# Attention scores issued two steps ahead, with another order and another pace of the projection products between them

## The chip, the cores and the metric

The kernel runs on one core of a Trainium2 chip. The time is the device time of one execution in microseconds (us); of several runs the median counts. The engines are named as in the profile: PE (TensorE matmuls), PEld (its weight loads), DVE (VectorE), ACT (ScalarE), POOL (GpSimd), SP (SyncE, which here only issues DMAs). Each engine works through its own instructions in the order in which they stand.

## The reference, cut to what matters

One attention layer and then one convolution layer over 1024 latent tokens with 1024 channels, plus 256 context tokens. The attention layer, which the change is in, has 16 query heads in 4 groups; the 4 heads of a group share one key and one value head of width 128:

```python
proj = h_lat @ w_in                                   # q | k | v | z
q = apply_rope(split_heads(proj[..., :q_end], 16), cos, sin)
k = apply_rope(split_heads(proj[..., q_end:k_end], 4), cos, sin)
# block of 128 queries: keys of the blocks before, at and after it (|i-j| <= 128), all 256 context keys, a sink
p_ctx, p_win = sink_softmax(sink_l, s_ctx, s_win)
o = p_ctx @ vc + p_win @ vw
y = (o * jax.nn.silu(z)) @ w_out
```

Everything is f32. The kernel splits each f32 operand into a high and a low part and makes each product of three matmuls (high with high, high with low, low with high).

## The kernel before, in words

**Stages.** The kernel first normalises and modulates the tokens and projects head 0 (to about 110 us of the profile), then runs the attention loop (to about 890 us), then the output projection, the convolution layer and the final norm. PE's order is the order of the code, instruction by instruction. The order on DVE, ACT, POOL and SP is set by a scheduler when the kernel is built, which also picks which of two PSUM buffers a `pss` tile gets.

**A step.** The loop walks over 128 steps (h, b): head h of 16, query block b of 8. Three pieces of PE work belong to a step, and I write them S, T and pv:

- S(h, b), `scores`: six matmuls `pss<-kh/kl/kvc,qh/ql` that need the rotated queries `qh`, `ql` of head h. Behind them come DVE (the masked maximum, `CUSTOM_DVE ... p_page<-pss`), ACT (`exp`), DVE (reciprocal) and POOL (the scaling), which leave the probabilities in a page `p`.
- T(h, b), `transposes`: up to five transposes `pss<-ident,p_page`, which ACT and DVE copy out as `pthi` and `ptlo`.
- pv(h, half), `pv`: 21 matmuls `pso<-pthi/ptlo,...` after every fourth block. DVE multiplies the result by the gate `zs` of that half.

Before, step (h, b) issues S of the next step, then 12 filler products, then pv if one is due, then T(h, b). So a score is issued one step ahead of its transposes.

**Filler products.** A filler product is one 128x512 matmul `psg<-hh/hl,whi/wlo` of the projection of a later head. A "chunk" is 128 columns of `w_in`, two halves of 512 tokens, 24 products each. Chunk z(h) makes the gate of head h, chunk q(h) its queries. A half of q is not ready when its products are: `rope` copies it out on ACT, two DMAs on ACT's queue swap its halves, POOL and DVE multiply and add, ACT writes `qh`, POOL writes `ql`. Each chunk's weights come by one 512 KB DMA into a page `wraw` and are split by ACT (`whi`) and POOL (`wlo`) while the chunk before them is at work.

At the first block of a head the loop enqueues the chunks that the next head needs, and `fill(n)` takes n products from the queue. The first head of a group must take z(h), q(h+1) and also z(h+1), q(h+2); the last enqueues nothing. `fill(1000, ("q", h + 1))` empties the queue up to the next head's queries before that head's first score. At the end of a group ("regroup") the chunks k and v of the next group run in one piece, then S of the new group's first step.

**Other work in the loop.** `low_parts` (`lows`), from head 1 on, loads 512 KB of an output weight per item into a page `low`, has ACT and POOL take its low part (`lhi`, `low_page<-low_page,lhi_half`) and writes it back by DMA. `ada_rest` adds up the modulation vectors of the next layer on DVE (`mask_page`). All pages (`p`, `q`, `z`, weights, `low`) come from one pool of 45, first in, first out; a page handed out again waits for its last reader.

Of the kernel before, what the change touches and what calls it, by code (L numbers as in the profile page):

```python
# [14 lines left out]
P = 128  # L15
# [4 lines left out]
NH = 16  # L20
NG = 4
HD = 128
AW = NH * HD
KW = NG * HD
# [6 lines left out]
TB = T // P  # L31

ADA_FP = ((0, 0),)
FILL = 12
DEFER = 6
EARLY = 2
FIRST = 5
# [57 lines left out]
def backbone_kernel(  # L95
# [154 lines left out]
    def wcol(c0):  # L250
        return W[:, c0:c0 + P]
# [7 lines left out]
    def add_chunk(key, src):  # L259
        cidx[key] = len(chunks)  # L260
        chunks.append(src)
# [1 line left out]
    for key, src in (("k", 0), wk[0]), (("q", 0), wcol(0)), (("v", 0), wv[0]):  # L263
        add_chunk(key, src)
    for h in range(NH):
        add_chunk(("z", h), wcol(AW + 2 * KW + h * P))
        if h + 1 < NH:
            add_chunk(("q", h + 1), wcol((h + 1) * P))
        if h % 4 == 3 and h + 1 < NH:
            add_chunk(("k", h // 4 + 1), wk[h // 4 + 1])  # L270
            add_chunk(("v", h // 4 + 1), wv[h // 4 + 1])
# [526 lines left out]
    def finish(kind, n, half, o, d):  # L798

        sl = slice(half * 512, half * 512 + 512)  # L800
        if kind in "kv" and half == 2:
            c = kvt[n][2]
            if kind == "k":
                act(c[:, 0], o[:, 0:CT], AF.Copy)
                split_lo(V, c[:, 1], o[:, 0:CT], c[:, 0])
                return None
        if kind in "qk":
            return rope(o, sl, d[0][:, sl], d[1][:, sl], G if kind == "q" and n else V)
        if kind == "z":
            act(d[:, sl], o, AF.Tanh, scale=0.5)  # L810
            stt(d[:, sl], d[:, sl], 1.0, o, ALU.add, ALU.mult)
            return None
        w = CT if half == 2 else 512
        f = hp.alloc(F32, None, "vf")
        act(f[:, 0:w], o[:, 0:w], AF.Copy)

        def tail():
            if half == 2:
                vt_split(f, CT, *(c[:, i].rearrange("p (a b) -> p a b", b=P) for i in (2, 3)))
            else:  # L820
                vt_split(f, 512, *(t[:, half * 4:half * 4 + 4] for t in d))
            hp.free(f)

        return tail
# [24 lines left out]
    def job(key):  # L849
        kind, n = key  # L850
        i = cidx[key]
        wc = wsA.need(i)
        d = target(kind, n)
        wsA.load()
        late = None
        for half in PARTS[kind]:
            o = ps_g()
            gh = gemm_ctx(wc, o) if half == 2 else gemm_half(wc, half, o)
            for m, _ in enumerate(gh):
                yield  # L860
                if m == DEFER - 1 and late:
                    late()
            if half == PARTS[kind][0] and wsA.ns <= i + 1:
                wsA.split()
                wsA.load()
            late = finish(kind, n, half, o, d)
        if late:
            vlate[n] = late
        wsA.done(i)
        if key == ("v", NG - 1):  # L870
            for t in Hc:
                pg.free(*t)
# [8 lines left out]
    def fill(n, until=None):  # L881
        while n > 0 and fillq and until not in finished:
            try:
                next(fillq[0][1])
                n -= 1
            except StopIteration:
                finished.add(fillq.popleft()[0])

    def enqueue(key):
        fillq.append((key, job(key)))  # L890
# [56 lines left out]

    def pv(h, half):
        g = h // 4
        c, vh, vl = kvt[g][2:5]  # L950
        o = ps_o()
        q0 = half * 4
        work = [(*(c[:, n, i * P:i * P + P] for n in (2, 3)), slice(13 + 4 * i, 17 + 4 * i), slice(0, 512)) for i in range(2)]
        for kb in range(max(q0 - 1, 0), min(q0 + 4, TB - 1) + 1):
            qa, qz = max(kb - 1, q0), min(kb + 1, q0 + 3)
            b0 = 1 + 4 * (1 - (kb - qa)) + (qa - q0)
            n = qz - qa + 1
            if n == 1 and kb > qa:
                work.append((vh[:, kb], vl[:, kb], slice(0, 5, 4), slice(256, 512)))
            elif n == 1:  # L960
                work.append((vh[:, kb], vl[:, kb], slice(9, 22, 12), slice(0, 256)))
            else:
                work.append((vh[:, kb], vl[:, kb], slice(b0, b0 + 5 * (n - 1) + 1, 5),
                             slice((qa - q0) * P, (qz - q0 + 1) * P)))
        for n, (a, b, ps_, os_) in enumerate(work):
            last = n == len(work) - 1
            PE.matmul(o[:, os_], a, pthi[:, ps_], start=n == 0, stop=False)
            PE.matmul(o[:, os_], a, ptlo[:, ps_], start=False, stop=False)
            PE.matmul(o[:, os_], b, pthi[:, ps_], start=False, stop=last)
        sl = slice(half * 512, half * 512 + 512)  # L970
        oz = hp.alloc(F32, None, "oz")
        stt(oz[:, 0:512], o, 0.5, zt[h][:, sl], ALU.mult, ALU.mult)
        SY.dma_start(out=ozd[h, :, sl], in_=oz[:, 0:512])
        hp.free(oz)
        if half:
            pg.free(zt.pop(h))
            pg.free(*qt.pop(h))
# [45 lines left out]
    steps = [(h, qb) for h in range(NH) for qb in range(TB)]  # L1023
# [6 lines left out]
    tails.pop()()  # L1030
    for _ in range(2):
        next(adag)
    for i, (h, qb) in enumerate(steps):
        if qb == 0:
            for n in (() if h % 4 == 3 else (h + 1,) if h % 4 or not h else (h, h + 1)):
                enqueue(("z", n))
                if n + 1 < NH:
                    enqueue(("q", n + 1))
        if (h, qb) == (NH - 1, EARLY_FROM):
            run(lows)  # L1040
            for _ in range(EA + 1):
                next(projA)
            fillq.append((("wo", 0), early_proj()))
        if lstate[0] == "open" or h and (h % 4 < 3 or qb < LOWS):
            lstate[0] = next(lows, "shut")
        nxt = steps[i + 1] if i + 1 < len(steps) else None
        regroup = nxt and nxt[1] == 0 and nxt[0] % 4 == 0
        if nxt and nxt[1] == 0:
            fill(1000, ("q", h + 1))
        if nxt and not regroup:  # L1050
            scores(*nxt)
        if not regroup:
            fill(FILL)
        if pvq:
            pv(*pvq.popleft())
        if regroup:
            g = nxt[0] // 4
            old = kvt[g - 1]
            run(job(("k", g)))
            transposes(h, qb)  # L1060
            run(job(("v", g)))
            pv(h, 1)
            pg.free(*old)
            scores(*nxt)
            vlate.pop(g)()
            continue
        transposes(h, qb)
        if qb % 4 == 3:
            pvq.append((h, qb // 4))
        for _ in range(2 if qb == 1 or qb == 6 and h % 2 else 1):  # L1070
            next(adag, None)
# [577 lines left out]
```

## Time and profile before

| | us |
|---|---|
| median of 3 runs | 1788.18 |
| lowest and highest run | 1786.36, 1790.24 |
| the profiled execution | 1789.18 |
| its span, first to last instruction | 1787.4 |
| PE busy in the span | 1731.3 |

The profiled execution takes 1.8 us beyond its span, and lies 1.0 us over the median. A row of the timeline has start, duration, engine, line, operation, output `<-` inputs, and in brackets the idle time before it with what ended it. All instructions have line L89, a helper, so the names of the tiles tell the work apart. A matmul's duration overlaps the next one's; the distance between two starts is what a product costs. In a row of windows stand PE busy, PEld, DVE, ACT, POOL, the granted share of the TensorE clock (PEclk), the DMA engines' busy share and GB/s.

### The profile page before, as it was taken

What the parts mean: (1) busy time and instruction counts of PE and PEld (TensorE: products, weight loads), DVE (VectorE), ACT (ScalarE), POOL (GpSimd) and SP (SyncE); (2) the same over time, 40 slices, a digit from 0 to 9 for tenths busy, and PEclk for the clock granted to TensorE, in tenths of its full rate; (3) what the DMA queues carried; (4) which work ended last, traced back from release to release, by engine and by line L of the source; (5) the groups of instructions that cost most, each with busy time, mean ns of one, the idle gap of its engine ahead of it and who ended that gap; (6) DMA issues with size and microseconds to landing.
All of it is one profiled execution on the core that took longest, in us unless ns stands there. A gap on an engine that the chain in (4) does not pass through costs nothing.

```text
span 1787.4 us, 23804 instructions
## 1 busy us (share of the span) xinstructions
PE 1731.3 (97%) x8383; PEld 1428.6 (80%) x8383; DVE 1147.8 (64%) x2078; ACT 866.8 (48%) x1406; POOL 940.5 (53%) x844
## 2 busy tenths in 40 slices
PE   5899999999999999899999999999999999999997
PEld 3578888788887888788888888888888888788886
DVE  5755564556544654455514349999999999867823
ACT  5344443445444544444533435655656565466731
POOL 2345665566644665654200147998988889121300
PEclk8899999999999999899999999999999999999999
DMA  9324443345334443334787723111121212376971
GB/s 302 106 54 124 147 134 89 112 139 162 104 93 140 142 139 101 109 109 145 286 279 248 256 86 112 42 46 37 36 80 39 71 48 70 107 252 231 328 272 47
DMA packets 195324, 242.45 MB, mean 136 GB/s; under 512 B 11798, under 2 KB 126790, under 8 KB 195204
## 3 DMA queue, kind: packets, MB, share of 16 engines
q1 hardware_dynamic: 188516, 230.10, 39.4%
q10 hardware_dynamic: 6688, 10.83, 2.5%
q8 instruction: 66, 1.08, 0.2%
q14 instruction: 54, 0.44, 0.1%
HBM read 188.70 MB, written 41.69 MB: 129 GB/s over the span
## 4 chain that ended last, share of the span: by engine, by line
PE 91%; DMA 3%; DVE 2%; issue 1%; ACT 1%; POOL 1%; SPq 0%; ACTq 0%; POOLq 0%; DVEq 0%
PE psg L89 46%; PE pss L89 23%; PE pso L89 21%; DMA rope_half<-rope_half 1%; DMA low_page<-in_conv_w_out_dram 1%; DVE alo_page L89 1%; SPq L89 0%; DMA araw_page<-in_ada_w_dram 0%; DMA ozd<-oz_half 0%; DVE ptlo L89 0%; DMA ozf_page<-ozd 0%; DMA x_page<-in_x_dram 0%; POOL ql_page L89 0%; DMA low_page<-in_attn_w_out_dram 0%; DVE hf_page L89 0%
## 5 line engine op out<-in xcount | busy, mean ns | idle before, releaser
L89 POOL TENSOR_TENSOR odd_half<-odd_half,prod_half 128x513 f32<-128x513 f32 (+2 forms) x252 | 313.4, 1252 | 24.1 <-ACT prod_half L89 10.9
L89 PE MATMUL psg<-hh_page,whi_page 128*128 128x512 f32 x600 | 240.9, 402 | 0.3 <-DVE kvc_page L89 0.3
L89 PE MATMUL psg<-hh_page,wlo_page 128*128 128x512 f32 x600 | 239.6, 399 | 0.0
L89 PE MATMUL psg<-hl_page,whi_page 128*128 128x512 f32 x600 | 239.4, 399 | 0.0
L89 POOL TENSOR_TENSOR wlo_page<-wraw_page,whi_page 128x1024 fp32r<-128x1024 f32 x72 | 179.6, 2496 | 98.8 <-ACT whi_page L89 74.3
L89 ACT ACTIVATE prod_half<-ubuf,dww 128x513 f32<-128x513 f32 (+2 forms) x252 | 165.1, 675 | 110.6 <-POOL odd_half L89 107.9
L89 PE MATMUL psg<-h2h_page,whi_page 128*128 128x512 f32 x464 | 184.1, 397 | 0.0
L89 PE MATMUL psg<-h2l_page,whi_page 128*128 128x512 f32 x464 | 182.7, 394 | 0.0
L89 PE MATMUL psg<-h2h_page,wlo_page 128*128 128x512 f32 x464 | 182.6, 393 | 0.0
L89 POOL TENSOR_SCALAR p_page<-p_page,sc 128x640 f32<-128x640 f32 (+1 forms) x128 | 101.1, 790 | 149.2 <-DVE sc L89 148.2
L89 DVE SCALAR_TENSOR_TENSOR pss<-ubuf,dww,pss 128x512 f32<-128x512 f32 (+3 forms) x270 | 172.5, 671 | 0.1
L89 DVE SCALAR_TENSOR_TENSOR pss<-ubuf,wsum,pss 128x512 f32<-128x512 f32 (+3 forms) x270 | 171.8, 671 | 0.2
L89 ACT ACTIVATE pthi<-pss 128x640 fp32r<-128x640 f32 (+1 forms) x144 | 89.0, 618 | 126.9 <-PE pss L89 120.3
L89 ACT ACTIVATE p_page<-p_page,sc 128x641 f32<-128x641 f32 (+1 forms) x128 | 102.9, 804 | 96.9 <-DVE sc L89 91.6
L89 DVE TENSOR_TENSOR ptlo<-pss,pthi 128x640 fp32r<-128x640 f32 (+1 forms) x144 | 103.3, 718 | 67.2 <-ACT pthi L89 66.2
L89 PEld LDWEIGHTS psg<-hh_page,wlo_page 128*128 128x128 f32 x600 | 114.5, 191 | 27.1
L89 PEld LDWEIGHTS psg<-hh_page,whi_page 128*128 128x128 f32 x600 | 114.8, 191 | 21.6 <-DVE kvc_page L89 0.7
L89 PEld LDWEIGHTS psg<-hl_page,whi_page 128*128 128x128 f32 x600 | 114.9, 192 | 21.0
L89 ACT ACTIVATE whi_page<-wraw_page 128x1024 fp32r<-128x1024 f32 x88 | 92.7, 1053 | 64.6 <-PE psg L89 28.4
L89 PE MATMUL pso<-h2h_page,whi_page 128*128 128x512 f32 x304 | 119.7, 394 | 0.0
L89 PE MATMUL pso<-h2l_page,whi_page 128*128 128x512 f32 x304 | 119.7, 394 | 0.0
L89 PE MATMUL pso<-h2h_page,wlo_page 128*128 128x512 f32 x304 | 119.6, 394 | 0.0
(235 smaller groups left out, 4111.7 us busy)
## 6 DMA issues: line engine op xcount, KB each, us to landing
wraw_page<-in_conv_w_in_dram SPq DMA_DIRECT2D x48, 512.0 KB
wraw_page<-in_attn_w_in_dram SPq DMA_DIRECT2D x40, 512.0 KB
wo_page<-in_attn_w_out_dram SPq DMA_DIRECT2D x32, 512.0 KB
wol_page<-wolA SPq DMA_DIRECT2D x32, 512.0 KB
wo_page<-in_conv_w_out_dram SPq DMA_DIRECT2D x32, 512.0 KB
wol_page<-wolC SPq DMA_DIRECT2D x32, 512.0 KB
rope_half<-rope_half ACTq DMA_DIRECT2D x80, 128.0 KB
araw_page<-in_ada_w_dram SPq DMA_DIRECT2D x32, 256.0 KB
```

The costliest lines, as they stand in the source:

```text
L89: r = f(*a, **k)
```

## The change

S moves one step further ahead: step (h, b) issues the score of two steps later, S(0, 1) goes ahead of the loop, and at a regroup two scores are issued. The next head's queries must therefore be ready a step earlier, at block 6 instead of 7. In group 0, and for the last head of every group, the queue's order stays z then q; for the other heads from head 4 on, q comes before z, and `pv` takes products one by one if its gate half has none behind it yet. A step has 12 filler products in group 0, 15 in the first head of a later group and 11 in the others.

```diff
-FILL = 12
+FILL = (12, 15, 11)
...
+        zq = [(("z", h), wcol(AW + 2 * KW + h * P))]
         if h + 1 < NH:
-            add_chunk(("q", h + 1), wcol((h + 1) * P))
+            zq.insert(1 if h < 4 or h % 4 == 3 else 0, (("q", h + 1), wcol((h + 1) * P)))
+        for key, src in zq:
+            add_chunk(key, src)
...
             late = finish(kind, n, half, o, d)
+            ready.add((kind, n, half))
...
     def pv(h, half):
+        while ("z", h, half) not in ready:
+            fill(1)
...
+    scores(0, 1)
     for i, (h, qb) in enumerate(steps):
...
-                enqueue(("z", n))
-                if n + 1 < NH:
-                    enqueue(("q", n + 1))
+                for key in ((("z", n), ("q", n + 1)) if n < 4 or n % 4 == 3 else (("q", n + 1), ("z", n))):
+                    if key[1] < NH:
+                        enqueue(key)
...
-        if nxt and nxt[1] == 0:
+        ahead = steps[i + 2] if i + 2 < len(steps) else None
+        if ahead and ahead[1] == 0:
             fill(1000, ("q", h + 1))
-        if nxt and not regroup:
-            scores(*nxt)
+        if ahead and ahead[0] // 4 == h // 4:
+            scores(*ahead)
         if not regroup:
-            fill(FILL)
+            fill(FILL[0 if h < 4 else 1 if h % 4 == 0 else 2])
...
             scores(*nxt)
             vlate.pop(g)()
+            scores(*ahead)
             continue
```

PE has 7708 rows before and after: none is added, all the difference is in their order. Three places show it; numbers in the names tell the buffers apart.

The first is PE ahead of the first score of head 5, S(5, 0), the second head of group 1. Before, `psg_223` is the second half of q(5) and the score (`qh_page_233`) stands right behind its last product:

```order
L89 MATMUL psg_223_3143<-hh_page_93_528,wlo_page_228_2929 128x512
L89 MATMUL psg_223_3143<-hh_page_97_555,whi_page_227_2928 128x512
L89 MATMUL psg_223_3143<-hl_page_98_556,whi_page_227_2928 128x512
L89 MATMUL psg_223_3143<-hh_page_97_555,wlo_page_228_2929 128x512
L89 MATMUL pss_225_3192<-kh_page_210_2566,qh_page_233_3016 128x256
```

Now the products ahead of it (`psg_217`) are those of z(4), and both halves of q(5), which is `qh_page_225`, stand far above:

```order
L89 MATMUL psg_217_3083<-hh_page_83_465,wlo_page_229_2914 128x512
L89 MATMUL pss_222_3153<-ident_66,p_page_233_3001 128x128 x5
L89 MATMUL pso_223_3161<-ones_71,mask_page_111_631 128x1 x2
L89 MATMUL pss_224_3171<-kh_page_210_2566,qh_page_225_2858 128x256
L89 MATMUL pss_224_3171<-kvc_page_212_2568,qh_page_225_2858 128x256
```

Between the last product of q(5)'s first half and S(5, 0) stand 24 products of the second half, one score and two sets of transposes before, and 66 products, four scores, five sets of transposes and one pv now.

The second place is PE at the loop's start. Before, the filler products of z(0) (`psg_64`) follow S(0, 1), which is `pss_66`:

```order
L89 MATMUL pss_66_1011<-kh_page_115_690,ql_page_119_694 128x384
L89 MATMUL pss_66_1011<-kvc_page_117_692,ql_page_119_694 128x256
L89 MATMUL psg_64_978<-hh_page_93_528,whi_page_131_907 128x512
L89 MATMUL psg_64_978<-hl_page_94_529,whi_page_131_907 128x512
L89 MATMUL psg_64_978<-hh_page_93_528,wlo_page_132_908 128x512
```

Now S(0, 2), `pss_68`, stands between them:

```order
L89 MATMUL pss_66_1011<-kh_page_115_690,ql_page_119_694 128x384
L89 MATMUL pss_66_1011<-kvc_page_117_692,ql_page_119_694 128x256
L89 MATMUL pss_68_1025<-kh_page_115_690,qh_page_118_693 128x384
L89 MATMUL pss_68_1025<-kvc_page_117_692,qh_page_118_693 128x256
L89 MATMUL pss_68_1025<-kl_page_116_691,qh_page_118_693 128x384
L89 MATMUL pss_68_1025<-kvc_page_117_692,qh_page_118_693 128x256
L89 MATMUL pss_68_1025<-kh_page_115_690,ql_page_119_694 128x384
L89 MATMUL pss_68_1025<-kvc_page_117_692,ql_page_119_694 128x256
L89 MATMUL psg_64_978<-hh_page_93_528,whi_page_131_907 128x512
```

The built program gives `pss_66` and `pss_68` the same PSUM buffer, so the second waits until DVE has read the first. Before, S(0, 2) stood 12 products and T(0, 0) later and had the other buffer.

The third place is ACT, on the way from q(5)'s first half to `qh`. Before, the work behind the copy of the half (`rope_half_84`) holds a low part (`lhi_half_93`), and the copy of the second half:

```order
L89 ACTIVATE rope_half_84_3132<-psg_214_3018 128x512
L89 ACTIVATE pthi_73<-pss_219_3094 128x5x128
L89 DMA rope_half_85_3133<-rope_half_84_3132 64x512 x2
L89 ACTIVATE p_page_237_3119,sc_222_3120<-p_page_237_3119,sc_222_3120 128x513
L89 ACTIVATE pthi_73<-pss_224_3156 128x5x128
L89 ACTIVATE lhi_half_93_3344<-low_page_244_3295 128x512
L89 ACTIVATE rope_half_88_3181<-psg_223_3143 128x512
L89 ACTIVATE whi_page_246_3311<-wraw_page_229_2932 128x1024
L89 ACTIVATE qh_page_233_3016<-rope_half_86_3134 128x512
```

Now:

```order
L89 ACTIVATE rope_half_80_2919<-psg_202_2860 128x512
L89 DMA rope_half_81_2920<-rope_half_80_2919 64x512 x2
L89 ACTIVATE pthi_73<-pss_207_2937 128x5x128
L89 ACTIVATE lhi_half_89_3120<-low_page_232_2992 128x512
L89 ACTIVATE p_page_231_2960,sc_209_2961<-p_page_231_2960,sc_209_2961 128x641
L89 ACTIVATE qh_page_225_2858<-rope_half_82_2921 128x512
```

A low part stands ahead of `qh` in both. At the regroups PE now has S of the new group's first block, four transposes of v, and then S of the second and third block in a row, where the third has the first one's PSUM buffer.

More of the change, by code (lines that the diff above doesn't have):

```diff
@@ L265, in backbone_kernel @@
     for h in range(NH):
-        add_chunk(("z", h), wcol(AW + 2 * KW + h * P))
+        zq = [(("z", h), wcol(AW + 2 * KW + h * P))]
         if h + 1 < NH:
-            add_chunk(("q", h + 1), wcol((h + 1) * P))
+            zq.insert(1 if h < 4 or h % 4 == 3 else 0, (("q", h + 1), wcol((h + 1) * P)))
+        for key, src in zq:
+            add_chunk(key, src)
         if h % 4 == 3 and h + 1 < NH:
@@ L887, in fill @@
                 finished.add(fillq.popleft()[0])
+    ready = set()
     def enqueue(key):
```

## The prediction

> **What bounds the kernel now.** I read the page first, for the engine that the time hangs on.
>
> ```profile
> PE 1731.3 (97%) x8383; PEld 1428.6 (80%) x8383; DVE 1147.8 (64%) x2078; ACT 866.8 (48%) x1406; POOL 940.5 (53%) x844
> ...
> PE 91%; DMA 3%; DVE 2%; issue 1%; ACT 1%; POOL 1%; SPq 0%; ACTq 0%; POOLq 0%; DVEq 0%
> ```
>
> PE is busy for 97% and carries 91% of the chain that ended last. The change removes no PE work, so it can only win or lose PE's waits, and what the clock loses behind them. PE's waits from 200 to 800 us, which is most of the attention loop (total, times, longest), are few:
>
> ```profile
> PE pss L89 <- ACT qh_page L89: 10.8, 3, 3.9
> PE pss L89 <- POOL ql_page L89: 3.2, 3, 2.4
> PE psg L89 <- DVE rope_half L89: 0.9, 1, 0.9
> ```
>
> No wait there names a page `p`: scores one step ahead already hide the softmax, and two steps alone gain nothing. Three scores wait for rotated queries, 14.0 us in all. The windows of 5 us around them show where, and a second loss:
>
> ```profile
> 345.00:350.00 5.00, 2.42 (x11) 1.63 (x9) 2.42 (x3) 1.72 (x4) 3.87 (x5) 1.00 0.41 131
> 350.00:355.00 5.00, 3.56 (x11) 2.88 (x12) 1.25 (x3) 3.00 (x5) 3.45 (x3) 0.57 0.24 52
> 355.00:360.00 5.00, 5.00 (x22) 4.17 (x21) 0.90 (x3) 1.43 (x4) 4.89 (x5) 0.75 0.26 105
> ...
> 545.00:550.00 5.00, 2.66 (x12) 1.84 (x10) 1.88 (x2) 1.76 (x4) 3.79 (x5) 1.00 0.49 143
> 550.00:555.00 5.00, 2.90 (x10) 2.40 (x11) 1.45 (x3) 3.02 (x5) 3.23 (x3) 0.71 0.22 52
> 555.00:560.00 5.00, 5.00 (x19) 4.02 (x19) 0.16 (x1) 1.62 (x4) 4.37 (x5) 0.61 0.27 108
> ...
> 745.00:750.00 5.00, 2.75 (x12) 1.88 (x10) 2.38 (x5) 1.67 (x3) 5.00 (x6) 1.00 0.63 176
> 750.00:755.00 5.00, 1.76 (x6) 1.47 (x7) 0.00 (x0) 1.92 (x4) 3.29 (x5) 0.51 0.17 38
> 755.00:760.00 5.00, 5.00 (x14) 3.91 (x13) 0.92 (x3) 1.34 (x3) 3.87 (x4) 0.50 0.00 0
> ```
>
> PE busy (second number) falls short of the window by 4.0, 4.4 and 5.5 us, and behind each gap the granted clock is 0.50 to 0.75. The timeline of the first, on PE, ACT and POOL:
>
> ```profile
> 347.02 0.40 PE L89 MATMUL psg<-hh_page,wlo_page 128*128 128x512 f32 x1
> 351.28 0.58 PE L89 MATMUL pss<-kh_page,qh_page 128*128 128x256 f32 x1 [3.86 <-ACT qh_page L89]
> ...
> 339.64 0.60 ACT L89 ACTIVATE rope_half<-psg 128x512 f32<-128x512 f32 x1 [0.27 <-PE psg L89]
> ...
> 348.65 0.63 ACT L89 ACTIVATE lhi_half<-low_page 128x512 fp32r<-128x512 f32 x1 [3.28 <-DMA low_page<-in_attn_w_out_dram]
> ...
> 350.61 0.62 ACT L89 ACTIVATE qh_page<-rope_half 128x512 fp32r<-128x512 f32 x1
> ...
> 351.31 1.30 POOL L89 TENSOR_TENSOR ql_page<-rope_half,qh_page 128x512 fp32r<-128x512 f32 x1 [2.44 <-ACT qh_page L89]
> ```
>
> This is S(5, 0), behind q(5)'s last product. The first half of q(5) was copied out at 339.64; its `qh` stands on ACT behind a low part that waits for its page, and ends at 351.23, `ql` at 352.61: 13.0 us, while PE had 7.4 us of work (339.64 to 347.02). The usual way is shorter, and the other heads give it more. For head 1:
>
> ```profile
> 141.57 0.60 ACT L89 ACTIVATE rope_half<-psg 128x512 f32<-128x512 f32 x1 [1.57 <-PE psg L89]
> ...
> 148.62 1.54 POOL L89 TENSOR_TENSOR ql_page<-rope_half,qh_page 128x512 fp32r<-128x512 f32 x1 [0.74 <-ACT qh_page L89]
> ...
> 155.69 0.39 PE L89 MATMUL pss<-kh_page,qh_page 128*128 128x256 f32 x1
> ```
>
> That is 8.6 us to the end of `ql` at 150.16, of 14.1 to the score. So the three waits belong to heads 5, 9 and 13, whose queries stand behind 48 products of z in a queue that starts empty.
>
> **The change part by part.** The sum is made against the profiled execution, 1789.18 us (span 1787.4); the median of 1788.18 lies 1.0 lower.
>
> *Queries ahead of the gate, 15 products a step.* One undisturbed step of PE, by the starts of its parts, prices the work: 12 products, a pv, T, S, and the next product.
>
> ```profile
> 328.96 0.39 PE L89 MATMUL psg<-hh_page,whi_page 128*128 128x512 f32 x1
> ...
> 331.74 0.39 PE L89 MATMUL pso<-pthi,kvc_page 128*128 128x512 f32 x1
> ...
> 335.25 0.71 PE L89 MATMUL pss<-ident,p_page 128*128 128x128 f32 x5
> 335.71 0.42 PE L89 MATMUL pss<-kh_page,qh_page 128*128 128x384 f32 x1
> ...
> 336.67 0.39 PE L89 MATMUL psg<-hh_page,whi_page 128*128 128x512 f32 x1
> ```
>
> A product costs 2.78 / 12 = 0.232 us, a pv 3.5, T 0.5, S 1.0. q(5) is now the first chunk. Between its first half and S(5, 0) lie 66 products, four scores, five sets of transposes and a pv: 15.3 + 4.0 + 2.5 + 3.5 = 25 us, against the 13.0 of the worst case. The same holds for heads 9 and 13, and heads 6, 7, 10, 11, 14, 15 get 28 to 31 us by the same count. So 4.0 + 4.4 + 5.5 = 14.0 us of idle time go. The slow clock behind them costs busy time times what was withheld: 3.56 x 0.43 + 5 x 0.25 = 2.8; 2.90 x 0.29 + 5 x 0.39 = 2.8; 1.76 x 0.49 + 5 x 0.50 = 3.4. That is 8.9 us, an estimate. Together -22.9.
>
> *The gate behind.* pv now needs z's half from later in the queue. At pv(4, 0) 75 products are taken, 72 needed; at pv(6, 0) two too few, which `fill(1)` takes earlier. The same products run; PE does not read `zs`. Cost 0. A moved chunk takes its weight DMA and ACT's and POOL's split along; at the rates above it has two chunks of lead, over 20 us.
>
> *Scores earlier: the start.*
>
> ```profile
> 117.56 0.42 PE L89 MATMUL pss<-kh_page,qh_page 128*128 128x384 f32 x1
> ...
> 118.53 0.39 PE L89 MATMUL psg<-hh_page,whi_page 128*128 128x512 f32 x1
> ...
> 124.69 0.44 PE L89 MATMUL pss<-kh_page,qh_page 128*128 128x384 f32 x1 [2.78 <-DVE rope_half L89]
> ...
> 119.61 0.88 DVE L89 CUSTOM_DVE_ANT_0 p_page<-pss,mask_page,nsink 128x640 f32<-128x640 f32 x1
> ...
> 125.00:130.00 5.00, 5.00 (x18) 4.07 (x17) 2.31 (x5) 1.55 (x3) 2.56 (x3) 0.66 0.09 26
> ...
> 1530.00:1535.00 5.00, 3.52 (x14) 2.29 (x13) 3.48 (x8) 0.69 (x1) 0.00 (x0) 1.00 0.15 56
> ```
>
> S(0, 2) waited 2.78 us for a PSUM buffer of head 0's projection, and 5 x 0.34 = 1.7 us of clock followed: 4.5. Now it stands at 118.53 and waits for the maximum of S(0, 1), which ends at 120.49: 2.0 us, with 12 products, T(0, 0) and S(0, 3) queued behind. S(0, 3) needs what S(0, 2) needed, free by 124.69, and comes at 120.5 + 1.0 + 2.8 + 0.5 = 124.8. Whether 2.0 us cost clock lies between two rows: 1.48 us idle in the window at 1530 (1.00) and 2.78 (0.66). It is nearer to the first: I take -2.5, with -0.8 if the dip stays. The Trainium skill, "TensorE: Matmul & The Clock Gate", Part 1, says the clock halves after about 3.4 us idle in a free-running window; the row of 2.78 us shows less can do it, and by the page's figure the term would be -2.5 too.
>
> *Scores earlier: heads 1 to 3.* In group 0 z still leads. S(1, 0) now comes 10.8 us behind the first half (14.1 before), S(2, 0) and S(3, 0) 12.3 by the same count. Against 8.6 us: 0. Against 13.0: waits of 2.2, 0.7 and 0.7, the upper end.
>
> *The regroups.*
>
> ```profile
> 309.84 0.28 PE L89 MATMUL pss<-kh_page,qh_page 128*128 128x256 f32 x1
> ...
> 310.90 0.42 PE L89 MATMUL pss<-kh_page,qh_page 128*128 128x384 f32 x1
> ...
> 311.88 0.39 PE L89 MATMUL psg<-hh_page,whi_page 128*128 128x512 f32 x1
> ...
> 310.86 0.75 DVE L89 CUSTOM_DVE_ANT_0 p_page<-pss,mask_page,nsink 128x512 f32<-128x512 f32 x1
> ```
>
> S(4, 2) moves to 311.88 and needs the buffer of S(4, 0), whose maximum is done at 311.61. Cost 0; were DVE a copy later (0.75), 0.5 us, three times.
>
> *The unseen rest.* 15 products a step fill an accumulator faster than its readers were used to; the nearest row is the one wait of 0.9 on `rope_half` above. I add one: +0.9 (0 to 2.7).
>
> Sum: -22.9 - 2.5 + 0.9 = -24.5, so 1764.7 for an execution like the profiled one, and 1763.7 against the median.
>
> **The rivals.**
>
> *Pages run short (the other side).* A score two steps ahead holds one more page, and queries taken early hold two for longer. Counted along the code, 2.8 to 4.2 pages are free on average in the later groups (5.0 to 5.2 before), and at two places none. S(3, 7), S(7, 7) and S(11, 7) get a page that a low part gave back 5.7 to 6.1 us of PE work earlier; before, the shortest such lead was 10.6. That page is still being written to DRAM, and DVE must wait with everything behind it, the copies that free PE's buffers included.
>
> ```profile
> SPq L89 <- POOL low_page L89: 72.7, 17, 12.3
> ...
> 338.76 0.18 POOL L89 COPY p_page<-nsink 128x1 f32<-128x1 f32 x1 [3.13 <-DMA wolA<-low_page]
> ```
>
> POOL already waited 3.1 us for such a page. A wait costs up to 10.6 - 5.7 = 4.9 us, and 2.8 of clock: 7.7. One gives 1771.4, three 1786.8, and a fourth is the point from which it is slower. Against it: T now comes a step (4 us) later behind its score, and before, DVE's maxima waited for DMAs in about as many places of the program (14, now 15) with no wait of PE. The same page's section on the array says that ACT and DVE are strictly first in, first out, which speaks for this rival; the trace agrees, with `qh` behind the low part above.
>
> *Heads 1 to 3 wait.* 2.2 + 0.7 + 0.7 and one dip of 2.8 bring 1770.1. Against it: no low part runs in head 0, and those held `qh` up.
>
> *The waits stay*, because something else holds `qh` for 25 us: only the start changes, 1786. Nothing in the trace takes half as long.
>
> **How the numbers follow.** The forecast has 0.74, heads 1 to 3 0.09, one page wait 0.08, three 0.04, the waits that stay 0.02, slower by pages 0.03. The predicted time is the forecast's, 1763.7. Its low end is every gain and no new wait (22.9 + 4.5 + the 0.9 of `rope_half` = 28.3, so 1759.9); the high end takes in heads 1 to 3 and one page wait with its neighbours, 1775. A difference of 0.2% (3.6 us) is about what a measurement tells from none: faster has 0.91, the same 0.06 (three page waits, and the waits that stay), slower 0.03.
>
> **What would show it.** In the profile after: no wait on `qh` or `ql`; PEclk 1.00 in every window of the loop past 140 us; a wait at the loop's start of about 2 us, whose releaser is DVE's `p_page`; PE busy within 1% of before. The prediction is wrong if PE waits for `p_page`, or DVE in the loop for `wolA<-low_page` with a row of PE behind it.

## The result, and the profile after

The changed kernel takes 1775.65 us in the median of four runs (1774.82 to 1779.90), against 1788.78 us before in the same set. The ratio is 0.9933, 95% interval 0.9913 to 0.9952. It is faster by 13.1 us. The forecast was 24.5 us, to 1763.7; its range ended at 1775.0, just under the median. The sign was right, nearly half of the gain was missing. One run of all those below, of the kernel with another start, ran at a granted clock of 0.75 (2130.42 us) and is left out of its median.

The profiled execution (1779.9 us, span 1778.1) lies 4.2 us above its median. The engines' busy times, and PE's waits from the loop's start to the last score:

```profile
PE 1726.9 (97%) x8383; PEld 1424.5 (80%) x8383; DVE 1157.8 (65%) x2078; ACT 864.0 (49%) x1406; POOL 941.0 (53%) x844
```

```profile
PE pss L89 <- DVE sc L89: 7.9, 5, 3.1
PE pso L89 <- DVE ptlo L89: 1.8, 4, 0.9
PE pss L89 <- DVE ptlo L89: 1.5, 3, 0.8
PE psg L89 <- DVE rope_half L89: 1.1, 1, 1.1
PE pss L89 <- POOL p_page L89: 0.8, 2, 0.4
```

No wait names `qh` or `ql`: the 14.0 us are gone. In their place stand 13.1 us of others, where before there were 4.0 beside the three: nearly all are scores, transposes and pv that wait for DVE's `sc` and `ptlo`, which is the softmax being late. The two largest, 2.84 us at the start and 3.05 us at 848 us, cost clock as well. Windows of 3.41 us (PE busy is the second number, PEclk the third from the end):

```profile
120.58:124.00 3.42, 1.48 (x9) 1.40 (x10) 2.55 (x6) 1.81 (x4) 0.99 (x3) 1.00 0.00 0
124.00:127.41 3.41, 3.41 (x10) 2.63 (x9) 2.15 (x5) 1.52 (x3) 3.03 (x3) 0.50 0.34 79
844.21:847.62 3.41, 1.05 (x7) 0.37 (x5) 1.40 (x2) 2.00 (x2) 0.20 (x1) 1.00 1.03 395
847.62:851.03 3.41, 2.72 (x9) 2.53 (x10) 2.77 (x6) 3.23 (x5) 0.43 (x1) 0.50 0.73 287
851.03:854.45 3.42, 3.42 (x10) 2.65 (x9) 2.92 (x6) 3.12 (x6) 0.83 (x3) 0.50 0.70 209
```

What each late softmax hangs on can be read from the timeline, at three places. At the loop's start (PE, then DVE, then ACT):

```profile
119.40 0.28 PE L89 MATMUL pss<-kvc_page,ql_page 128*128 128x256 f32 x1
122.52 0.44 PE L89 MATMUL pss<-kh_page,qh_page 128*128 128x384 f32 x1 [2.84 <-DVE sc L89]
...
120.97 0.69 DVE L89 TENSOR_TENSOR vl_page<-pso,vh_page 128x512 fp32r<-128x512 f32 x1 [5.12 <-ACT vh_page L89]
121.58 0.88 DVE L89 CUSTOM_DVE_ANT_0 p_page<-pss,mask_page,nsink 128x640 f32<-128x640 f32 x1
...
119.86 0.60 ACT L89 ACTIVATE rope_half<-pss 128x512 f32<-128x512 f32 x1 [3.20 <-DMA rope_half<-rope_half]
```

S(0, 2) waits for the maximum of S(0, 1). That maximum stands on DVE behind the split `vl`, that behind ACT's `vh`, and that behind a copy that waits on ACT for rope's DMA until 119.86. So it ends at 122.46, not at 120.49 as before. Of these 2.0 us 1.0 is the opening, which as a whole ended that much later in this profile; for the rest, ACT waited 3.20 us for rope's DMA in place of 2.12. In group 0, head 2 (SP, ACT, PE):

```profile
210.38 0.42 SPq L89 DMA_DIRECT2D wolA<-low_page  x1
213.93 0.38 SPq L89 DMA_DIRECT2D low_page<-in_attn_w_out_dram  x1
...
218.16 1.15 ACT L89 ACTIVATE lhi_half<-low_page 128x512 fp32r<-128x512 f32 x2 [3.84 <-DMA ozd<-oz_half]
219.22 0.82 ACT L89 ACTIVATE p_page<-p_page,sc 128x641 f32<-128x641 f32 x1
...
222.28 0.74 PE L89 MATMUL pss<-ident,p_page 128*128 128x128 f32 x5 [1.38 <-DVE sc L89]
```

The load of a low part at 213.93 has waited on SP since 210.80. SP's list of waits for 205 to 224 us says for what, in total, times, longest:

```profile
SPq L89 <- DMA wolA<-low_page: 3.0, 1, 3.0
```

The page it gets is that of a low part which is still being written out. The part lands late, ACT stands 3.84 us before it (the part landed at 218.14; the row names a second releaser, a half page being written, whose write ended at about the same time), and the `exp` of a score stands behind it. The wait of 0.9 us of a pv at 209 us is of another kind: the copy `ptlo` that it needs stands on DVE behind two rows of modulation vectors (`mask_page`) and the gate. At the loop's end (ACT, DVE, PE):

```profile
845.14 1.06 ACT L89 ACTIVATE ozh_page<-ozf_page 128x1024 fp32r<-128x1024 f32 x1 [4.74 <-DMA ozf_page<-ozd]
...
846.23 1.22 DVE L89 TENSOR_TENSOR ozl_page<-ozf_page,ozh_page 128x1024 fp32r<-128x1024 f32 x1 [4.17 <-ACT ozh_page L89]
847.37 0.88 DVE L89 CUSTOM_DVE_ANT_0 p_page<-pss,mask_page,nsink 128x640 f32<-128x640 f32 x1
...
848.31 0.69 PE L89 MATMUL pss<-kh_page,qh_page 128*128 128x384 f32 x1 [3.05 <-DVE sc L89]
```

Here the operands of the early output projection are the late ones: their loads leave SP in one bunch from 837.74 us on (DMA share 1.03 in the window above), and DVE has their split ahead of the maximum that PE's score buffer hangs on.

### The profile page after: what moved, and what is told of

It is laid out like the page before. It is cut to its first block, busy times and chain, and to the rows that moved or that the text cites. A ratio compares the mean times of both kernels' runs of the same rounds, so it can differ in the third digit from the quotient of the medians.

```text
span 1778.1 us, 23767 instructions
## 1 busy us (share of the span) xinstructions
PE 1726.9 (97%) x8383; PEld 1424.5 (80%) x8383; DVE 1157.8 (65%) x2078; ACT 864.0 (49%) x1406; POOL 941.0 (53%) x844
## 3 DMA queue, kind: packets, MB, share of 16 engines
q8 instruction: 66, 1.08, 0.2%
## 4 chain that ended last, share of the span: by engine, by line
PE 61%; DMA 2%; DVE 1%; POOL 1%; ACT 1%; issue 0%; ACTq 0%; DVEq 0%; SPq 0%; POOLq 0%
PE psg L89 30%; PE pss L89 16%; PE pso L89 16%; DMA rope_half<-rope_half 1%; DMA ozf_page<-ozd 0%; POOL rope_half L89 0%; DMA wo_page<-in_conv_w_out_dram 0%; DMA low_page<-in_conv_w_out_dram 0%; DMA wolC<-low_page 0%; DMA dww_raw<-in_ada_w_dram 0%; POOL wlo_page L89 0%; ACT woh_page L89 0%; DVE pss L89 0%; DVE x_page L89 0%; DVE p_page L89 0%
## 5 line engine op out<-in xcount | busy, mean ns | idle before, releaser
L89 DVE CUSTOM_DVE_ANT_0 p_page<-pss,mask_page,nsink 128x640 f32<-128x640 f32 (+1 forms) x112 | 96.2, 859 | 36.7 <-PE pss L89 28.5
```

Of the source, the lines that this page charges most:

```text
L89: r = f(*a, **k)
```

## The experiments

My theory after the comparison was that the queue's order brings the whole gain, and that the other two parts of the change (scores two steps ahead, 15 and 11 products a step) take some of it back because pages run short. The rivals: the losses belong to one unlucky profile; or they come with the order; or the work's order on DVE and ACT is at fault and not the pages.

All runs in one table, by pieces of their profiles. "Opening" ends where the last transpose `pso<-ident,vf_half` before the loop starts, each group with the same row of the next regroup, "group 3 and projection" with the first product of `h2h_page`. "Against before" is the median less that of the kernel before on the same chip.

| kernel | opening | group 0 | group 1 | group 2 | group 3 and projection | rest | median | against before |
|---|---|---|---|---|---|---|---|---|
| before | 117.5 | 193.4 | 200.2 | 200.1 | 344.3 | 731.8 | | |
| changed | 118.5 | 197.8 | 193.5 | 195.2 | 342.4 | 730.8 | 1775.65 | -13.1 |
| e1 changed, again | 118.3 | 195.9 | 192.7 | 195.4 | 340.1 | 731.7 | 1775.13 | -11.8 |
| e8 order alone | 116.6 | 193.9 | 194.2 | 193.7 | 338.5 | 731.7 | 1770.49 | -16.5 |
| e11 order alone | 117.0 | 191.8 | 194.0 | 192.2 | 338.7 | 732.0 | 1769.27 | -17.4 |
| e2 order, 15 and 11 | 118.8 | 193.3 | 197.4 | 194.1 | 336.4 | 732.0 | 1773.69 | -13.2 |
| e12 order, 15 and 11 | 116.5 | 193.8 | 198.6 | 193.9 | 336.5 | 731.8 | 1773.95 | -12.7 |
| e10 order, two steps | 117.7 | 197.1 | 193.7 | 193.4 | 337.4 | 732.7 | 1771.89 | -14.8 |
| e3 two steps alone | 116.6 | 195.3 | 199.4 | 199.7 | 345.3 | 732.4 | 1793.20 | +6.3 |
| e4 changed, other start | 117.0 | 198.9 | 193.3 | 196.0 | 339.9 | 731.9 | 1778.70 | -8.2 |
| e5 two steps in groups 1, 2 | 116.4 | 193.4 | 194.2 | 195.9 | 336.0 | 732.3 | 1771.21 | -15.8 |
| e9 the same, 12 products | 115.2 | 193.5 | 197.0 | 192.6 | 339.7 | 731.5 | 1771.90 | -14.8 |
| e7 as e5, 24 products first | 117.5 | 196.3 | 193.1 | 195.5 | 336.3 | 733.1 | 1773.18 | -13.9 |
| e6 changed, no low parts in group 0 | 117.7 | 190.2 | | | | | | |
| e14 as e2, no low parts in group 1 | | | 192.9 | | | | | |
| e13 order alone, 44 pages | 120.1 | 191.1 | 200.3 | 201.1 | 339.7 | 732.7 | 1786.73 | +0.4 |

### Is the first profile typical?

> The changed kernel once more, nothing edited. In its first profile the score at 848 us waited 3.05 us behind read-backs of the output projection's operands, with half clock behind it. Theory A (the wait belongs to the order of the code): a wait of 2.5 to 3.5 us and a PEclk of 0.5 to 0.9 near 848 us again, time 1775 to 1780. Theory B (it hangs on when a few transfers land, and the first profile was an unlucky one, 4.2 us above the median of its runs): no wait over 1.5 us between 830 and 870 us, PEclk 1.00 there, a span near 1773.

Median 1775.13, ratio 0.9931 (0.9916 to 0.9946), span 1774.1. Each theory had half of it. The waits are there again, 2.21 us at the start and 2.65 us at 845 us, so they belong to the code. The clock behind them is not halved this time. Both waits straddle two windows of the clock's grid, which leaves each over half busy:

```profile
120.36:123.77 3.41, 2.10 (x11) 1.92 (x12) 2.92 (x7) 1.45 (x3) 0.99 (x3) 1.00 0.08 20
123.77:127.19 3.42, 3.42 (x20) 2.97 (x20) 2.02 (x4) 1.79 (x4) 3.06 (x3) 1.00 0.25 59
840.57:843.98 3.41, 2.15 (x12) 1.24 (x10) 0.69 (x1) 1.78 (x2) 0.39 (x2) 1.00 1.04 407
843.99:847.40 3.41, 2.03 (x11) 1.85 (x12) 2.78 (x5) 2.75 (x6) 0.00 (x0) 1.00 0.95 368
847.40:850.81 3.41, 3.12 (x19) 2.49 (x17) 3.26 (x7) 3.41 (x6) 0.94 (x2) 1.00 0.86 278
```

### The parts of the change by themselves

The order alone: the queries ahead of the gate, one step ahead, `FILL = (12, 12, 12)`. With the pace: the same with `(12, 15, 11)`. Both are the changed kernel with

```diff
-    scores(0, 1)
...
-        if ahead and ahead[1] == 0:
+        if nxt and nxt[1] == 0:
             fill(1000, ("q", h + 1))
-        if ahead and ahead[0] // 4 == h // 4:
-            scores(*ahead)
+        if nxt and not regroup:
+            scores(*nxt)
...
-            scores(*ahead)
             continue
```

> Queries ahead of the gate and 15 or 11 products a step, as in the change, but scores one step ahead as before. Theory A (the queries bring the whole gain; scores two steps ahead bring new waits in group 0 and at the loop's end): the start and group 0 as before (193.4 us from the first vf transposes to the second), groups 1 and 2 at 193 to 195, no dip of the clock near 848 us; time 1788.8 - 14.0 - 8.9 + 0.9 = 1766.8, between 1765 and 1769. Theory B (the new waits come with the queries' order and the pace of 15 products): group 0 as before, but the end waits as in the changed kernel; 1772 to 1776.

> Queries ahead of the gate in the later groups, scores one step ahead, and 12 products a step everywhere as before. Theory A (the order of the queue is what removes the waits on rotated queries): no wait on qh or ql, groups 1 to 3 as with 15 and 11 products within 1.5 us, the time within 2 us of 1773.7. Theory B (the order alone leaves the gate late and the pace of 15 is needed): waits on the gate or on drained queues of 1 us or more appear in heads 4, 8 and 12, and the time is over 1777.

With the pace: 1773.69, ratio 0.9925 (0.9910 to 0.9940). Start, group 0 and the end are as theory A said, with no dip at the end; but group 1 is 197.4 us for at most 195, and the time is outside A's range, inside theory B's, and within 1.5 us of the changed kernel's. The order alone: 1770.49, ratio 0.9900 (0.9875 to 0.9925). The order is what removes the waits, as theory A said; but the time lies 1.2 us below A's range, and group 1 and the last piece differ from those with the pace by 3.2 and 2.1 us, where A allowed 1.5. PE's waits of the loop in that kernel, the largest five:

```profile
PE pss L89 <- DVE rope_half L89: 3.3, 1, 3.3
PE pss L89 <- POOL p_page L89: 1.6, 1, 1.6
PE psg L89 <- DVE zs_page L89: 1.5, 1, 1.5
PE pss L89 <- DVE ptlo L89: 1.2, 4, 0.4
PE pss L89 <- DVE sc L89: 0.6, 1, 0.6
```

The first is the old wait at the start; the loop behind it has lost its large ones. The next two are new against the kernel before: the first transposes behind the last regroup wait for their probabilities (704 us), and a product of the early projection for an accumulator that the gate has not left yet (843 us). The two kernels had run on different chips, so they were run side by side, five times each:

> The queue's order alone (queries ahead of the gate, 12 products, one step ahead) once more, beside the same with 15 and 11 products, on one chip, in more rounds: 1770.5 and 1773.7 us came from different calls. Theory A (the pace of 15 and 11 costs by itself): 1769.5 to 1771.5 here, 2 to 4 us under the other. Theory B (the difference was the opening's, which lay between 116.4 and 118.8 us in nine profiles whatever the kernel): within 1.5 us of the other.

> Queries ahead of the gate with 12, 15 and 11 products, one step ahead: the other half of the comparison. Theory A: 1773 to 1775, 2 to 4 us over the order alone, with group 1 at 196 to 198 against 194. Theory B: within 1.5 us of the order alone, both near 1771 to 1773.

1769.27, ratio 0.9903 (0.9888 to 0.9919), and 1773.95, ratio 0.9927 (0.9915 to 0.9940). Theory A: the pace costs 4.7 us here and 3.2 us before, and all nine runs of the order alone (1767.4 to 1772.2) lie under all nine with the pace (1772.4 to 1775.0). The loss is in group 1 (198.6 against 194.0); some 2 us come back in the last piece. At 365 us, with 15 products (the timeline of SP, ACT, POOL, DVE and PE, and the windows):

```profile
355.30 0.33 SPq L89 DMA_DIRECT2D wolA<-low_page  x1
...
360.71 0.89 SPq L89 DMA_DIRECT2D low_page<-in_attn_w_out_dram  x2
...
362.96 0.63 ACT L89 ACTIVATE qh_page<-rope_half 128x512 fp32r<-128x512 f32 x1 [5.59 <-POOL rope_half L89]
...
365.12 0.63 ACT L89 ACTIVATE lhi_half<-low_page 128x512 fp32r<-128x512 f32 x1 [1.26 <-DMA low_page<-in_attn_w_out_dram]
...
359.61 1.29 POOL L89 TENSOR_TENSOR rope_half<-rope_half,sin_page 128x512 f32<-128x512 f32 x1 [4.02 <-DMA rope_half<-rope_half]
...
364.24 0.87 DVE L89 CUSTOM_DVE_ANT_0 p_page<-pss,mask_page,nsink 128x640 f32<-128x640 f32 x1
...
365.27 0.74 PE L89 MATMUL pss<-ident,p_page 128*128 128x128 f32 x5 [1.27 <-DVE sc L89]
366.53 0.44 PE L89 MATMUL pss<-kh_page,qh_page 128*128 128x384 f32 x1 [0.53 <-DVE ptlo L89]
```

```profile
363.68:367.09 3.41, 1.61 (x10) 1.09 (x9) 2.04 (x5) 2.15 (x5) 1.26 (x1) 1.00 0.80 299
367.09:370.50 3.41, 3.41 (x12) 2.83 (x11) 2.69 (x4) 2.83 (x6) 2.86 (x4) 0.50 0.14 38
```

Two chains meet here. The larger wait, 1.27 us, ends with DVE's maximum of 364.24. That stands behind `ptlo` on DVE and `pthi` on ACT, and these behind ACT's `qh`, which waits 5.59 us for POOL's part of rope. POOL waits for rope's two DMAs: issued from 353.49 us on, the second landed at 359.48, while the weights of the next chunk and a low part's write, issued at 353.60 and 355.30, were under way. With the order alone, where those weights had landed before, the same two landed 2.9 us behind the first one's issue and not 6.0. The smaller wait, 0.53 us, is the pattern of group 0: the load of a low part stands on SP until the write of 355.30 has landed, ACT waits 1.26 us for it, and `pthi` and `ptlo`, which PE waits for, stand behind it. Both fall into one window, and the clock halves behind it.

Scores two steps ahead, with the queue and the 12 products of before, and then with the new order and 12 products (the edit is that of the first, against the kernel before; the second is the changed kernel with `FILL = (12, 12, 12)`):

```diff
+    scores(0, 1)
...
-        if nxt and not regroup:
-            scores(*nxt)
+        if ahead and ahead[0] // 4 == h // 4:
+            scores(*ahead)
...
             vlate.pop(g)()
+            scores(*ahead)
```

> Scores two steps ahead as in the change, but the gate ahead of the queries and 12 products a step everywhere, as before. Theory A (alone it only brings waits): the first score of heads 5, 9 and 13 comes a step (4 to 8 us of PE work) earlier against the same rotation, so those three waits grow from 4.0, 4.4 and 5.5 to 8 or more, group 0 is 3 to 5 us longer; 1800 to 1815. Theory B (the score's distance is neutral, and drained queues give the work back later): 1786 to 1792.

> The changed kernel with 12 products a step everywhere in place of 12, 15 and 11. Theory A (scores two steps ahead cost in group 0 and at the loop's end, whatever the pace): group 0 at 196 to 198, a wait of 2 to 3 us on a score near 845, 1773 to 1776. Theory B (the pace made the loop's end and the middle tight, two steps are free): 1769 to 1771.

Two steps alone: 1793.20, ratio 1.0038 (1.0025 to 1.0050), slower than before. The time lies under theory A's range and 1.2 us over B's. A was right that group 0 gets longer (1.9 us, where it said 3 to 5) but wrong on the three waits: they shrank to 1.9 us each (1.32 + 0.62 at 349 us, 1.26 + 0.62, 1.20 + 0.61), and other waits on `sc`, 1.5 to 1.9 us each in groups 1 and 2, took their place. At the loop's end it has a wait of 2.25 us (856 us) with a halved window. Why the three shrank was not followed up.

Two steps with the order: 1771.89, ratio 0.9915 (0.9900 to 0.9930), between the two theories and 2.6 us over the order alone on the same chip, though the runs of the two overlap. Theory A holds for group 0 (197.1), which is 5.3 of the 6.4 us between the two profiles; the wait near 845 us is 0.4 to 0.5 us and not 2 to 3. So with the new order the changed kernel's wait at the loop's end needs both two steps and the pace.

### Where two steps cost, and where they might pay

In the changed kernel, the first step's products ahead of its score:

```diff
-        if ahead and ahead[0] // 4 == h // 4:
+        if i and ahead and ahead[0] // 4 == h // 4:
             scores(*ahead)
         if not regroup:
             fill(FILL[0 if h < 4 else 1 if h % 4 == 0 else 2])
+        if not i:
+            scores(*ahead)
```

> The changed kernel, with one thing moved: in the loop's first step the 12 products stand ahead of the score of step 2, not behind it. Theory A (the wait of 2.84 us at the start only comes from where that score stands): no wait over 0.5 us and PEclk 1.00 from 118 to 140 us, 2.8 + 1.7 = 4.5 us less than the changed kernel: 1771. Theory B (VectorE is late as a whole there, and what comes next, the transposes of step 0 or the score of step 3, waits as long): 1775 to 1776, the wait moved to 122 to 127 us.

1778.70, ratio 0.9952 (0.9935 to 0.9968): theory B, and worse. The wait moved to 122.85 us (1.08) and 124.74 us (1.25), both in one window of the clock, which halved behind them. The first is released by POOL's scaling of the probabilities, the second by DVE's part of rope.

Two steps in groups 1 and 2 alone; the same with 12 products; and the first with 24 products in the loop's first step:

```diff
+TWO = (1, 2)
...
-    scores(0, 1)
...
-        ahead = steps[i + 2] if i + 2 < len(steps) else None
+        dist = 2 if h // 4 in TWO else 1
+        ahead = steps[i + dist] if i + dist < len(steps) else None
...
-            scores(*ahead)
+            if g in TWO:
+                scores(*steps[i + 2])
```

> The changed kernel, with scores two steps ahead in groups 1 and 2 alone and one step ahead in groups 0 and 3 (nothing of it moves in the first step). Theory A (two steps cost in group 0 and at the loop's end, where pages are short, and pay in group 1, where softmax is late behind other work): the pieces of the traces add up, in the order opening, group 0, 1, 2, the rest of the loop with the projection, and the remainder: 118.3 + 193.3 + 192.9 + 195.2 + 336.4 + 732.0 = 1768.1 of span, so about 1770 in the median. Theory B (what group 0 or the end lost comes back elsewhere, since the same transfers must be placed): 1773 to 1776.

> Queries ahead of the gate, 12 products a step everywhere, scores two steps ahead in groups 1 and 2 alone. Theory A (12 products and two steps in the middle each spare what the change lost there): groups 1 and 2 at 193 and 194, the rest as with the order alone (span 1768.5), so 1769 to 1770. Theory B (with 12 products two steps bring the waits on pages back in the middle): groups 1 and 2 over 195 each, 1772 or more.

> As the kernel with two steps in groups 1 and 2 alone, and 24 products in the loop's first step in place of 12. Theory A (VectorE is late once, after the opening; 2.8 us of products taken earlier cover it): the wait of 2.7 us near 125 us falls under 0.5 with no dip behind it, 3.5 to 4.5 us less than without: 1766. Theory B (the 12 products are missed at the end of group 0, whose queue runs dry a step earlier): the wait goes, and as much comes back before the regroup at 311 us; no difference over 1.5 us.

The first: 1771.21, ratio 0.9903 (0.9882 to 0.9925), span 1768.2 for a forecast of 1768.1, theory A. With 12 products: 1771.90, ratio 0.9917 (0.9903 to 0.9932), group 1 at 197.0, nearer to B. So with the pace, two steps in the middle save most of what the pace costs there (group 1 at 194.2 in place of 197.4 and 198.6); without the pace they save nothing in this kernel. A piece does not stand by itself, though: with two steps everywhere and 12 products group 1 takes 193.7 us, and of the 197.0 here 1.7 are one halved window at 369 us. With 24 products first: 1773.18, ratio 0.9917 (0.9896 to 0.9938), nearer to theory B and 2.0 us worse than without: the wait at the start is down to 0.60 us, but waits of 1.15 us at 222 us and 2.31 us at 278 us appear, the second with a halved window, and group 0 is 2.9 us longer.

None of these beats the order alone, which has the lowest time found; two steps in groups 1 and 2 cannot be told from it (intervals 0.9882 to 0.9925 and 0.9875 to 0.9925).

### Are pages the cause?

No low parts during group 0 in the changed kernel; no low parts during group 1 in the kernel with order and pace (all of them are still made, the rest at the loop's end, which is disturbed by it and not read):

```diff
-        if lstate[0] == "open" or h and (h % 4 < 3 or qb < LOWS):
+        if lstate[0] == "open" or h > 3 and (h % 4 < 3 or qb < LOWS):
...
+        if lstate[0] == "open" or h and h // 4 != 1 and (h % 4 < 3 or qb < LOWS):
```

> The changed kernel, with no low parts during heads 1 to 3; they begin with head 4 and what is left of them runs in one go at the loop's end. Only group 0 is read. Theory A (two-step scores hold a page more, so a low part's load waits for a page that is still being written, ScalarE waits for the load, and softmax and TensorE with it): the waits near 207, 220 and 263 us (0.9, 1.6, 0.5) go, and group 0 is 192.5 to 194.0 instead of 195.9 to 197.8. Theory B (the waits come from VectorE's own work, the modulation rows for one): the waits stay above 2 us in all and group 0 over 195.

> Queries ahead of the gate with 12, 15 and 11 products, one step ahead, and no low parts during group 1 (what is left of them runs in one go at the loop's end). Only group 1 is read: 197.4 and 198.6 us with them, 194.0 and 194.2 with 12 products. Theory A (ScalarE waits there for a low part whose page is still being written): the waits near 366 and 417 us (1.3 to 2.0 and 1.1) go, group 1 at 192 to 194. Theory B (15 products a step starve the softmax by themselves): the waits stay, group 1 over 196.

Theory A in both (one execution each). Group 0 went from 197.8 and 195.9 to 190.2 us, below A's range. Of this 2.7 and 0.4 us lie at the start, ahead of any low part: a wait of 1.85 us there and no halved window. The rest, 4.9 and 5.4 us, goes with the low parts. From 130 to 308 us PE has no wait that the profile lists; in the changed kernel there were these:

```profile
PE pss L89 <- DVE sc L89: 1.4, 1, 1.4
PE pso L89 <- DVE ptlo L89: 0.9, 1, 0.9
PE pss L89 <- DVE ptlo L89: 0.7, 2, 0.5
```

Group 1 went from 197.4 and 198.6 to 192.9 us. These two runs show that the low parts are behind the waits. They don't show that pages are what makes the low parts late: taking them out frees pages, transfers and work alike. In the second run rope's DMAs near 353 us, with neither the weights nor a write beside them, land 2.9 us behind the first one's issue again, and not 6.0, so the larger wait there goes with the transfers. To try the pages by themselves, one was taken from the kernel that does best, and nothing else changed:

```diff
-    pg = Pages(pgpool, 45, "page", 1024)
+    pg = Pages(pgpool, 44, "page", 1024)
```

> The queue's order alone (1769.3 and 1770.5 us), with 44 pages in place of 45 and nothing else. Theory A (pages are what two-step scores and the pace of 15 run short of): one page fewer brings the same waits, behind low parts that wait for a page still being written; group 0 or 1 longer by 2 us or more, 1772 to 1776. Theory B (the queue's order has a page to spare, the cost of the other parts is in the work's order on ScalarE and VectorE): 1769 to 1771.5.

1786.73, ratio 0.9999 (0.9990 to 1.0009). One page of 45 costs 17 us, the whole gain: theory A, at several times its price and only in part at its places. Group 0 is not longer, though SP waits there twice for a low part's write (4.6 us in all); groups 1 and 2 are, by 6 to 9 us each, and the opening by 3. PE's largest wait in the groups is that for a regroup's values; behind it are two rows of SP's waits in group 1:

```profile
PE pso L89 <- ACT vf_half L89: 6.3, 2, 3.2
```

```profile
SPq L89 <- POOL wlo_page L89: 23.0, 3, 15.5
...
SPq L89 <- DMA wolA<-low_page: 4.6, 1, 4.6
```

SP stands 15.5 us at one weight load, behind POOL's reading of a page; the order alone with 45 pages has no such wait in group 1, but one of 2.9 us for a low part's write. So this kernel has no page to spare, and which transfer becomes the late one differs from kernel to kernel; how the late weight load makes the regroup's values late was not followed further. Whether a page fewer costs the kernel before as much, and whether a page more gives the changed kernel its loss back, was not run: that pages are behind all of the loss stays unshown.

## Why the prediction was right or wrong

**The three waits (-14.0) and the clock behind them (-8.9): right in kind, nearly right in size.** With the order alone, groups 1 to 3 with the projection lose 6.0 + 6.4 + 5.9 = 18.3 us and 6.3 + 7.9 + 5.7 = 19.9 us in two profiles; I had 22.9. In the changed kernel the same pieces lose 6.8 + 4.9 + 1.9 = 13.6 us, and 16.5 in the second profile. What lacks there is what the other parts took back.

**The step that failed: new waits of the softmax were put at nothing.** The sum has the start, one wait of 0.9 us on `rope_half`, and no other new wait: pages were left to a rival, since "T now comes a step (4 us) later behind its score", and a softmax that is late for another reason was not considered. The two profiles of the changed kernel show, for `sc` and `ptlo`, waits of 3.0 and 3.2 us in group 0 behind the start, and of 4.4 and 4.1 us at the loop's end, in the first with two halved windows (3.1 us: half of 6.8 less 0.7 idle). The spans are 9.3 and 13.3 us shorter than before, 15.2 and 11.2 us short of the forecast. With the opening, 1.0 and 0.8 us later, and the start, 2.5 and 0.2 us dearer than I had it, these waits account for 14.0 of the 15.2 us and 8.3 of the 11.2.

**The start (-2.5): the wait as described, the clock left to chance.** S(0, 2) waits for the maximum of S(0, 1), 2.84 and 2.21 us in the two profiles, and 2.39, 2.12 and 1.85 in three other kernels with scores two steps ahead in group 0, for my 2.0. With the score one step ahead, 12 products first and 45 pages, the wait there is 2.7 to 3.3 us in eight profiles, 2.78 in that of before. The half clock followed the waits of 2.84 and 2.39 us and not the other three; in the first profile the start saved nothing, in the second 2.3 us. Opening and group 0 together still became 5.4 us longer, 3.4 in the second profile, by the opening and the waits named above.

**The gate (0), heads 1 to 3 (0), the regroups (0): right as they were meant.** No wait on `zs` from `pv`, on `qh` or `ql` anywhere, or on a score behind a regroup. Heads 1 to 3 do wait, but for the softmax.

**The unseen rest (+0.9): much too small as a price of the pace.** I added a second wait on `rope_half`; there is still one, 1.15 and 1.48 us for the 0.93 of before. I had looked only at who reads the accumulators. 15 products a step cost 3.2 and 4.7 us. At 365 us they cost it by rope's DMAs beside a weight load and a low part's write, and by a low part that waits for its page; for the other waits the cause stays open.

**The rival "pages run short" named the right page, and I gave it 0.15 in all.** In group 0 the page that it named, one of a low part still being written, is the one that is waited for. I put the wait on the wrong engine: I looked for DVE or POOL at a `p` page. POOL's waits for such pages, 12.6 us in seven from 120 to 860 us before, fell to 1.5 us in one. It was the next low part's load on SP that waited; then ACT, in order, with an `exp` behind it. Against the rival I had counted DVE's waits for DMAs, which says nothing of SP's. In the profile before SP never waits for `wolA<-low_page` from 120 to 860 us; in the changed one:

```profile
SPq L89 <- DMA wolA<-low_page: 8.7, 4, 3.0
```

Such a wait is not enough by itself: the order alone has one in group 1 (2.9 and 3.0 us), and PE no wait over 0.4 us there.

**Missed altogether: the loop's end.** The early projection reads back its operands there. Two steps and the pace together make their loads late: 3.05 us and two halved windows in one profile, 2.65 us and none in the other. Why the loads leave in one bunch was not followed.

**The signs named.** No wait on `qh` or `ql`: held. PEclk 1.00 past 140 us: not in the first profile. A wait of about 2 us at the start, released by DVE's maximum: held, with a dip in one profile of the two. PE within 1% busy: held (1726.9 against 1731.3). Of the two signs of being wrong, PE waited for `p_page` (0.8 us in two), and DVE waited once for `wolA<-low_page` (2.1 us, at a `mask_page`), with no wait of PE behind it.

The sum was also made against an execution 2.2 to 2.8 us slower than that kernel's later medians (1786.4 to 1787.0). And the range's high end is no sum of its terms: heads 1 to 3 (6.4) and one page wait (7.7) on top of 1763.7 make 1777.8, not 1775.

## What to carry to other kernels

When work is moved earlier in a kernel whose buffers come from one pool, count the pool first and ask of every load that shares it, background loads included, whose page it gets and whether that is still being written. A late background load costs PE nothing until an in-order engine puts the softmax behind it. Ask too what a faster queue's transfers now run beside. Try the parts of a change by themselves: here one part in three carried all of the gain, and the other two, added to hide waits, cost a fifth to a third of it (3.4 to 5.6 us of 16.5 and 17.4).

## What the runs showed of the hardware

The half clock follows a fixed grid. In each of the 16 profiles every stretch at 0.50 begins on one grid of 3.41 us, and all but the one that the kernel's end cuts off last a multiple of it. Taking PE's idle time, as the timeline's rows have it, per window of that grid, from 90 to 1720 us, all cases part cleanly: of 81 windows at full clock with 1.0 us or more idle, the 54 with up to 1.72 us were followed by full clock, the 27 with 1.80 us or more by half. A halved window was followed by another one when PE idled 0.61 us or more in it (13 cases), and by full clock at 0.22 or less (27). Two windows on either side of the limit, in the kernel with the other start and in that with two steps alone:

```profile
224.00:227.41 3.41, 1.69 (x11) 1.26 (x10) 2.98 (x3) 0.62 (x2) 2.34 (x3) 1.00 0.43 165
227.41:230.83 3.42, 3.42 (x18) 2.92 (x17) 2.40 (x6) 2.38 (x5) 0.80 (x1) 1.00 0.93 259
```

```profile
746.63:750.04 3.41, 1.60 (x9) 0.95 (x8) 0.69 (x1) 1.63 (x3) 2.39 (x3) 1.00 0.48 154
750.04:753.45 3.41, 3.41 (x10) 2.68 (x9) 0.85 (x3) 1.34 (x3) 1.36 (x2) 0.50 0.24 83
```

So a wait of 2 to 3 us costs half of one window (1.7 us) more, nearly twice that as at 848 us, or nothing, by how it falls on the grid: 2.73 us at the start of one run of the order alone (1.36 and 1.37 us in two windows) cost none, 1.27 + 0.53 us inside one window did. My rule in the prediction, by the length of a wait, can't be right for one execution. The Trainium skill, "TensorE: Matmul & The Clock Gate", Part 1, has the free-running window of about 3.4 us, and the traces agree; its idle gap of about 3.4 us is too long, since 1.80 us inside one window was enough in every case here.
